# A hybrid mixer step on one Trainium2 core: beta multiplied into the decays on GpSimd, wider VectorE products, shorter scale computation

## The chip, the cores and the metric

The kernel runs on one core of one Trainium2 chip. Its engines are TensorE (PE, matrix products; PEld is its weight load), VectorE (DVE), ScalarE (ACT), GpSimd (POOL) and SyncE (SP, which here issues DMA transfers). Each engine runs its own instructions in order; waits between engines are by semaphores. SBUF is the working memory, PSUM takes TensorE's results. The metric is the device time of one execution in microseconds.

## The reference

One layer of a hybrid backbone for 128 context tokens and 2048 sample tokens, model width 1024. The input is normed and modulated, then one projection feeds three branches; each is gated by SiLU of another projection, projected back, weighted by a sigmoid gate, and the sum goes through an output projection and a residual.

```python
qkv, beta, dec, z_a, u_b, v_b, z_b, x_c, z_c, gates = jnp.split(proj, points, axis=-1)
# A: chunked gated DeltaNet, forward and backward
m = eye + bc[..., :, None] * jnp.einsum('bnhik,bnhjk->bnhij', kc, kc) * dec_strict
sol = lax.linalg.triangular_solve(m, rhs, left_side=True, lower=True, unit_diagonal=True)
qk = jnp.einsum('bnhik,bnhjk->bnhij', qc, kc) * dec_incl
# B: spatial gating in chunks of 128 tokens
vn = rmsnorm(v, g_norm).reshape(B, n, CHUNK_B, G_B, CH_B)
vs = jnp.einsum('gpq,bnqgc->bnpgc', w_s, vn) + b_s.T[None, None, :, :, None]
o_b = u * vs.reshape(B, T, W_BR) * jax.nn.silu(z_b)
# C: Fourier mixing of x_c, times silu(z_c)
pb = jnp.einsum('btnw,nwd->btnd', br, w_branch)
merged = jnp.einsum('btnd,btnd->btd', jax.nn.sigmoid(gates), pb)
out = jnp.einsum('btd,de->bte', merged, w_out)
```

## The kernel before

All products of float32 data are made of float16 pairs (a high and a low half, three products per block). To make the halves of a weight tile, `converting` (L198) squares it on ScalarE (L209, with the sum per partition in `ss`), turns the sum into bfloat16 on VectorE (`widened`, L173), sums it over the partitions with a product by ones, and `scales` (L178) takes from the exponent bits of the result a power of two `s` and its inverse: a copy out of PSUM (L183), a shift (L185), and a multiply-add of integers for each (L186, L187). `w.inv` is the inverse times `isx`, the inverse scale of the normed input (L216). Then ScalarE writes the high half (L218) and VectorE the low one (L219). This is done for 93 weight tiles; `scales` alone also serves the input, the branches, the bounds of the delta branch and the 17 blocks before the output projection.

The stages, in order of time: modulation, the normed input and z_A (to about 120 us), the q/k/v projection with its short convolution and the decays (to about 440 us), V, U and z_B of branch B, x_C and z_C with the Fourier products, the gates and branch products (`merge`), and the output projection.

The delta branch runs beside these as a generator whose steps `Pace` releases in proportion to the products written, `delta` (L1079). For each of 17 chunks of 128 tokens, `prep` (L681) loads q, k, v and the decays `dc` (`decay_rows`, L761, one chunk ahead), norms k (`norm` L693, with the inverse square root on GpSimd, L698, and `tok`, L707), transposes it (L723), makes K K^T in PSUM, and for each of two directions multiplies it by beta and the decay, head by head (L738, four instructions), copies the diagonal blocks (L740), and splits the result into halves (L742, L743). The blocks `nd` leave through two DMA issues on GpSimd's queue (L748). Then the products of q and k take the decays (L754) and are split (L756, L757). `n_` and `q_` share three buffers of tag `n32`. Between chunks, `base_inverse` (L766) inverts the diagonal blocks of a group by many small VectorE operations (L787, L788). Then `scan` goes over the chunks in both directions with its chain of products.

In branch B, `spatial` (L1155) multiplies the normed values of a chunk by the spatial weights, and adds the bias per group (L1161, four instructions, in which the norm's weight `sgug(g)` multiplies the product, channel by channel on the partitions). The values themselves are scaled by the inverse root mean square before (L1188).

A scheduler orders the instructions of each engine from the program, by dependences and buffers; `tc.high_priority()` and `tc.issue_after()` guide it. So a change in one place can move instructions elsewhere.

Of the kernel before, what the change touches and what calls it, by code (L numbers as in the profile page):

```python
# [12 lines left out]
I32 = mybir.dt.int32  # L13
# [7 lines left out]
P = 128  # L21
# [90 lines left out]
def hybrid_flow_kernel(ctx: ExitStack, tc: tile.TileContext, x_prompt, x_sample, state_delta, c, c_ctx, ln_g, w_ada,  # L112
# [62 lines left out]
        V.tensor_copy(sb16, ss)  # L175
        return sb16

    def scales(ss, pl, tag, sb16=None):  # L178

        ps = bank(ps_x, [P, 1])  # L180
        mm(ps, ones16, widened(ss, pl, tag) if sb16 is None else sb16)
        t = sb(pl, [P, 4], tag)
        V.tensor_copy(t[:, 0:1], ps)  # L183
        h = t[:, 3:4].bitcast(I32)
        V.tensor_scalar(h, t[:, 0:1].bitcast(I32), 24, None, ALU.logical_shift_right)  # L185
        V.tensor_scalar(t[:, 1:2].bitcast(I32), h, -8388608.0, 204.0 * 8388608, ALU.mult, ALU.add)  # L186
        V.tensor_scalar(t[:, 2:3].bitcast(I32), h, 8388608.0, 50.0 * 8388608, ALU.mult, ALU.add)  # L187
        return t[:, 1:2], t[:, 2:3]

    def load_w(src, nkt, cols=P, hi=None, lo=None, tag="w", bufs=5):  # L190
        return convert(read_w(src, nkt, cols, tag), nkt, cols, hi, lo, tag, bufs)
# [6 lines left out]
    def converting(w, st, nkt, cols=P, hi=None, lo=None, tag="w", bufs=5):  # L198

        wpool = bwp[0] if tag == "b" else wp  # L200
        if tag == "z":
            hi, lo = [sb(p0p, [P, nkt, cols], n_, F16, bufs=4) for n_ in ("zhi", "zlo")]
        if tag == "v":
            hi, lo = [t[:, vfilled[0]] for t in v4]
            vfilled[0] += 1
        w.hi = sb(wpool, [P, nkt, cols], tag + "hi", F16, bufs=bufs) if hi is None else hi
        w.lo = sb(wpool, [P, nkt, cols], tag + "lo", F16, bufs=bufs) if lo is None else lo
        ss = sb(wp, [P, 1], "wss", bufs=4)
        A.activation(w.lo, st, AF.Square, accum_out=ss)  # L209
        yield  # L210
        sb16 = widened(ss, wp, "wsc")
        if wnext[0] < 11:
            yield
        s, inv = scales(None, wp, "wsc", sb16)
        w.inv = sb(wp, [P, 1], "winv", bufs=10)
        V.tensor_mul(w.inv, inv, isx)  # L216
        yield
        A.activation(w.hi, st, AF.Copy, scale=s)  # L218
        V.scalar_tensor_tensor(w.lo, st, s, w.hi, ALU.mult, ALU.subtract)  # L219
# [143 lines left out]
        V.tensor_copy(pc, pp)  # L363

    convw = lambda j, ct: pc[:, 8 + j * 12 + ct:8 + j * 12 + ct + 1]
    sgug = lambda g: pc[:, 44 + g:45 + g]
    ong = pc[:, 48:49]


# [44 lines left out]
    with tc.high_priority():  # L414
# [7 lines left out]
        A.activation(bnd[:, 1, :], sh.rearrange("p k g -> p (k g)"), AF.Square, scale=math.sqrt(2.0), accum_out=bss[:, 1:2])  # L422
        V.tensor_add(bss[:, 2:3], bss[:, 0:1], bss[:, 1:2])
        sx, isx = scales(bss[:, 2:3], cp, "xsc")
        V.tensor_scalar(ms, ms, sx, None, ALU.mult)
        V.tensor_scalar(sh, sh, sx, None, ALU.mult)

# [46 lines left out]
    def h3(ap):  # L474
        return ap.rearrange("p (h x) -> p h x", h=H)
# [205 lines left out]
    def prep(g, ci, t, nxt, held):  # L681
# [49 lines left out]
        pair = lambda t_, h: (t_[:, 0, hs(h)], t_[:, 1, hs(h)])  # L731
        for h in range(H):
            mm3(ps[:, hs(h)], pair(T, h), pair(T, h))
        nd = sb(d2, [P, 2, H, 32], "nd", bufs=2)
        for d in range(2):
            n_ = sb(d2, [P, WB], "n32", bufs=3)
            for h in range(H):
                V.scalar_tensor_tensor(n_[:, hs(h)], ps[:, hs(h)], beta[:, d, t, h:h + 1], dc[:, d, hs(h)], ALU.mult, ALU.mult)  # L738
            for B in range(4):
                A.copy(nd[32 * B:32 * B + 32, d], h3(n_)[32 * B:32 * B + 32, :, 32 * B:32 * B + 32])  # L740
            n16 = sb(d2, [P, 2, WB], "n16", F16, bufs=4)
            made = A.activation(n16[:, 0, :], n_, AF.Copy, scale=FS)  # L742
            V.scalar_tensor_tensor(n16[:, 1, :], n_, FS, n16[:, 0, :], ALU.mult, ALU.subtract)  # L743
            late([(nD[d][t], n16)], made)
            yield 1
# [6 lines left out]
        for d in range(2):  # L752
# [3 lines left out]
            made = A.activation(p16[:, 0, :], q_, AF.Copy, scale=1.0 / FS)  # L756
            V.scalar_tensor_tensor(p16[:, 1, :], q_, 1.0 / FS, p16[:, 0, :], ALU.mult, ALU.subtract)  # L757
            late([(qkD[d][t], p16)], made)
            yield 1

    def decay_rows(t):  # L761
        dc = sb(dq, [P, 2, WB], "dc", bufs=2)
        SY.dma_start(dc, decD[t])
        return dc

    def base_inverse(g):  # L766
        nt = len(GROUPS[g])
# [311 lines left out]
    def delta():  # L1079
        nonlocal dq  # L1080
        seq = [(g, ci, t) for g, ts in enumerate(GROUPS) for ci, t in enumerate(ts)]
        held = {1: rows(1, 16), 2: rows(2, 16), 0: rows(0, 16), "dc": decay_rows(16)}
        yield from bounds()
        base = iter(())
        for i_, (g, ci, t) in enumerate(seq):
# [58 lines left out]
    bsp = sb(bp, [P, 4, P], "bsp", bufs=1)  # L1144
    SY.dma_start(bsp, b_spatial[0].rearrange("g (o p) -> o g p", o=1).to_broadcast([P, 4, P]))
    wsT = sb(bp, [P, 4, P], "wsT", bufs=1)
    vw = getw(4, 3)
    ps = bank(ps_x, [P, 4, P])
    for g in range(4):
# [3 lines left out]
    for i in range(4):  # L1153
        V.tensor_copy(vinv[:, i:i + 1], vw[i].inv)
    def spatial(t, vn):  # L1155
        vs = sb(bp, [P, 4, P], "vs", bufs=4)
        ps = bank(ps_x, [P, 4, P])
        for g in range(4):
            mm(ps[:, g, :], vn[:, g, :], wsT[:, g, :])
        for g in range(4):  # L1160
            V.scalar_tensor_tensor(vs[:, g, :], ps[:, g, :], sgug(g), bsp[:, g, :], ALU.mult, ALU.add)  # L1161
        vout.append((t, vs))

    def vstore(made):
# [5 lines left out]
    for t in range(NCH):  # L1170
# [12 lines left out]
        rsqrt(ss, ss, 1.0 / WB, 1)  # L1183
        if vprev is not None:
            spatial(*vprev)
        if len(vout) > 2:
            vstore(made)
        V.tensor_scalar(vn, vn, ss, None, ALU.mult)  # L1188
        vprev = (t, vn)
        if t == 8:  # L1190
            SY.dma_start(cf, consts[:, _CF:_CW])
# [366 lines left out]
```

## Time and profile before

| what | value |
|---|---|
| runs: median (lowest to highest of 3) | 2199.03 us (2198.21 to 2199.14) |
| profiled execution: span from the first to the last instruction | 2198.9 us |
| mean granted clock of TensorE | 0.994 |
| moved by DMA | 365.04 MB, mean 166 GB/s |
| instructions L738 / L1161 / L1188 on VectorE | 136 / 68 / 17 |
| weight tiles converted | 93 |

The page of a profile gives each engine's busy time and its share of the span; further views give groups of instructions (line, engine, operation, output and inputs, shapes, count, busy us, mean ns of one, idle time of the engine before them and what ended it), who waited for whom, the busy time by stretch of time, and instructions in order of time. Durations of instructions that follow each other can overlap by a part, so several in a row take less than their sum. The lines that matter are in the prediction.

### The profile page before, as it was taken

The numbers are of one execution on the slowest core, as the hardware profiler recorded it, in microseconds if no ns is written. First come the engines' busy times: TensorE is split into PE (matmuls) and PEld (weight loads), VectorE is DVE, ScalarE is ACT, GpSimd is POOL, SyncE is SP. The second block draws the span as 40 slices with busy tenths as digits, with TensorE's granted clock in tenths as the row PEclk, the third lists the DMA queues.
The fourth block names the chain that finished last, engine by engine and source line by source line (L and its number), as shares of the span: only waits on it lengthen the run. The fifth ranks groups of instructions, "written<-read, shape, count | busy, mean of one in ns | idle before, by whom it ended". The sixth has DMA issues, their size and how long they took to land.

```text
span 2198.9 us, 41979 instructions
## 1 busy us (share of the span) xinstructions
PE 2133.4 (97%) x15990; PEld 1231.3 (56%) x15990; DVE 1297.7 (59%) x3085; ACT 1007.5 (46%) x2325; POOL 713.8 (32%) x861
## 2 busy tenths in 40 slices
PE   7999999999999999999899999999999999999998
PEld 3565444455555587878555556555655444444444
DVE  5746745479878796455665555756574444233454
ACT  3644644355555563344644445755553422222332
POOL 1421433223334322432312233255442222122553
PEclk9999999999999999999999999999999999999999
DMA  8434733167777654433655556766664544433542
GB/s 279 142 99 156 252 117 111 60 206 220 238 224 237 205 166 110 123 115 115 219 171 165 161 168 187 235 186 212 213 207 147 172 125 123 124 101 110 180 153 105
DMA packets 304275, 365.04 MB, mean 166 GB/s; under 512 B 39393, under 2 KB 215754, under 8 KB 302026
## 3 DMA queue, kind: packets, MB, share of 16 engines
q1 hardware_dynamic: 251690, 267.38, 40.5%
q0 software_dynamic: 12688, 51.27, 6.5%
q10 hardware_dynamic: 39696, 43.72, 5.8%
q8 instruction: 125, 2.05, 0.4%
q14 instruction: 76, 0.62, 0.1%
HBM read 234.67 MB, written 127.62 MB: 165 GB/s over the span
## 4 chain that ended last, share of the span: by engine, by line
PE 47%; DMA 6%; DVE 5%; ACT 3%; issue 1%; POOL 1%; SPq 0%; ACTq 0%; POOLq 0%; DVEq 0%
PE b L161 47%; DMA st<-br 2%; DMA wst<-in_w_branch_dram 1%; DMA wst<-in_w_in_dram 1%; DMA mt<-mrg 1%; DVE E L788 1%; DVE XB L787 1%; DMA ei<-XB 0%; DMA skn<-kv 0%; DMA br<-o 0%; ACT big L1336 0%; DMA XB<-nd 0%; ACT XB L793 0%; DVE big L1337 0%; DVE u L904 0%
## 5 line engine op out<-in xcount | busy, mean ns | idle before, releaser
L161 PE MATMUL b<-xh,whi 128*128 128x512 f16 (+1 forms) x1920 | 650.5, 347 | 7.7 <-DVE sg L1125 5.0
L161 PE MATMUL b<-xl,whi 128*128 128x512 f16 (+1 forms) x1920 | 650.8, 347 | 0.0
L161 PE MATMUL b<-xh,wlo 128*128 128x512 f16 (+1 forms) x1920 | 650.2, 347 | 0.4 <-DVE wlo L219 0.4
L161 PEld LDWEIGHTS <-whi 128*128 128x128 f16 x3904 | 356.4, 98 | 335.2 <-issue 13.7
L161 PEld LDWEIGHTS <-wlo 128*128 128x128 f16 x1952 | 191.1, 98 | 178.8 <-issue 1.3
L161 PE MATMUL b<-big,bhi 128*128 128x512 f16 (+1 forms) x960 | 250.5, 347 | 1.5 <-DVE big L1337 1.1
L1376 POOL TENSOR_TENSOR mrow<-mrow,sg 128x512 f32<-128x512 f32 (+1 forms) x80 | 95.0, 1187 | 288.4 <-DVE sg L1375 163.6
L161 PE MATMUL b<-big,blo 128*128 128x512 f16 (+1 forms) x480 | 163.3, 347 | 0.0
L1366 ACT ACTIVATE sg<-b,winv 128x512 f32<-128x512 f32 (+1 forms) x120 | 74.2, 619 | 153.9 <-PE b L161 153.4
L628 POOL TENSOR_TENSOR cy<-cy,raw 128x545 f32<-128x545 f32 (+1 forms) x48 | 74.5, 1580 | 184.4 <-ACT raw L627 184.4
L161 PEld LDWEIGHTS <-xh 128*128 128x128 f16 x1496 | 117.1, 98 | 29.9 <-issue 1.5
L161 PEld LDWEIGHTS <-bhi 128*128 128x128 f16 x960 | 87.0, 98 | 76.0 <-ACT big L1336 0.3
L175 DVE CAST wscb<-wss 128x1 bf16<-128x1 f32 x93 | 14.3, 154 | 190.9 <-ACT wlo L209 83.4
L1375 DVE SCALAR_TENSOR_TENSOR sg<-b,binv,sg 128x512 f32<-128x512 f32 (+1 forms) x80 | 53.4, 668 | 102.3 <-PE b L161 90.9
L860 POOL COPY T<-ES 32x256 f16<-32x256 f16 x68 | 28.5, 419 | 208.2 <-DMA ES<-ei 179.3
L161 PE MATMUL b<-whi,xl 128*128 128x128 f16 x544 | 93.0, 219 | 0.0
L161 PE MATMUL b<-whi,xh 128*128 128x128 f16 x544 | 93.0, 219 | 0.0
L161 PE MATMUL b<-wlo,xh 128*128 128x128 f16 x544 | 93.0, 219 | 0.0
L161 PE MATMUL b<-wohi,mh 128*128 128x512 f16 (+2 forms) x248 | 91.9, 372 | 0.6 <-ACT mh L1446 0.6
L161 PE MATMUL b<-wohi,ml 128*128 128x512 f16 (+2 forms) x248 | 91.7, 372 | 0.3 <-DVE ml L1447 0.3
L161 PE MATMUL b<-wolo,mh 128*128 128x512 f16 (+2 forms) x248 | 91.9, 372 | 0.0
L219 DVE SCALAR_TENSOR_TENSOR wlo<-wst,wsc,whi 128x1024 f16<-128x1024 f32 x52 | 72.4, 1396 | 31.6 <-ACT whi L218 31.3
(455 smaller groups left out, 4281.2 us busy)
## 6 DMA issues: line engine op xcount, KB each, us to landing
wst<-in_w_in_dram SPq DMA_DIRECT2D x60, 512.0 KB, 5.5
qkv<-cy POOLq DMA_DIRECT2D x12, 1089.0 KB, 5.2
st<-br SPq DMA_DIRECT2D x48, 256.0 KB, 4.6
mrow<-mrg SPq DMA_DIRECT2D x18, 512.0 KB, 4.0
mrow<-mrg SPq DMA_DIRECT2D x16, 576.0 KB, 4.5
mrg<-mrow POOLq DMA_DIRECT2D x16, 576.0 KB, 3.7
dc<-dec SPq DMA_DIRECT2D x17, 512.0 KB
kq<-qkv SPq DMA_DIRECT2D x34, 256.0 KB, 4.8
```

What stands on the lines that cost most here:

```text
L161: PE.matmul(out, l, r, start=start, stop=stop)
L175: V.tensor_copy(sb16, ss)
L219: V.scalar_tensor_tensor(w.lo, st, s, w.hi, ALU.mult, ALU.subtract)
L628: G.tensor_tensor(y[:, c0:c1], y[:, c0:c1], raw[:, 1 + c0:1 + c1], ALU.mult)
L787: V.tensor_tensor(t3, X3[:, 0:k, k:k + 1].to_broadcast([P, k, n_]), E3[:, k:k + 1, k:32].to_broadcast([P, k, n_]), ALU.mult)
L788: V.tensor_tensor(E3[:, 0:k, k:32], E3[:, 0:k, k:32], t3, ALU.subtract)
L860: G.tensor_copy(T16[rows(a0, b), :, :, b], ES[0:32, :, 2 * a0 + b, :, wT])
L1366: A.activation(sg, ps, AF.Sigmoid, scale=gw.inv)
L1375: V.scalar_tensor_tensor(sg, ps, binv[:, 1:2], sg, ALU.mult, ALU.mult)
L1376: G.tensor_tensor(mr, mr, sg, ALU.add)
```

## The change

Three parts.

1. `weighted` is new: two GpSimd products per chunk multiply the decays of both directions by beta (broadcast over 128 columns) into two `n32` tiles. It is called at the end of the chunk before, for the next one; `prep` then multiplies K K^T in PSUM by that tile in one instruction of 512 columns per direction, in place.
2. The norm's weight of branch B is loaded as a tile broadcast over the partitions (`sgb`) and multiplied into the values together with their scale; the spatial result then needs one addition of the bias over all four groups. `vs` has three buffers, and its store is issued when two are waiting.
3. The squares of a weight are summed straight into bfloat16, the exponent is shifted straight out of PSUM, and the inverse scale of the input is folded in as exponent bits (`xbits`), so that `w.inv` comes from the multiply-add itself.

```diff
-    def scales(ss, pl, tag, sb16=None):
+    def scales(ss, pl, tag, sb16=None, inv=None):
...
-        V.tensor_copy(t[:, 0:1], ps)
         h = t[:, 3:4].bitcast(I32)
-        V.tensor_scalar(h, t[:, 0:1].bitcast(I32), 24, None, ALU.logical_shift_right)
+        V.tensor_scalar(h, ps.bitcast(I32), 24, None, ALU.logical_shift_right)
         V.tensor_scalar(t[:, 1:2].bitcast(I32), h, -8388608.0, 204.0 * 8388608, ALU.mult, ALU.add)
-        V.tensor_scalar(t[:, 2:3].bitcast(I32), h, 8388608.0, 50.0 * 8388608, ALU.mult, ALU.add)
-        return t[:, 1:2], t[:, 2:3]
+        if inv is None:
+            inv = t[:, 2:3]
+            V.tensor_scalar(inv.bitcast(I32), h, 8388608.0, 50.0 * 8388608, ALU.mult, ALU.add)
+        else:
+            V.tensor_scalar(inv.bitcast(I32), h, 8388608.0, xbits, ALU.mult, ALU.add)
+        return t[:, 1:2], inv
...
-        ss = sb(wp, [P, 1], "wss", bufs=4)
-        A.activation(w.lo, st, AF.Square, accum_out=ss)
+        ss = sb(wp, [P, 1], "wss", BF16, bufs=4)
+        with nc.allow_low_precision(reason="the sum only sets a power of two"):
+            A.activation(w.lo, st, AF.Square, accum_out=ss)
         yield
-        sb16 = widened(ss, wp, "wsc")
         if wnext[0] < 11:
             yield
-        s, inv = scales(None, wp, "wsc", sb16)
         w.inv = sb(wp, [P, 1], "winv", bufs=10)
-        V.tensor_mul(w.inv, inv, isx)
+        s, _ = scales(None, wp, "wsc", ss, w.inv)
...
         sx, isx = scales(bss[:, 2:3], cp, "xsc")
+        xbits = sb(cp, [P, 1], "xbits")
+        V.tensor_scalar(xbits, isx.bitcast(I32), -77.0 * 8388608, None, ALU.add)
...
+        db = cur["db"]
         nd = sb(d2, [P, 2, H, 32], "nd", bufs=2)
         for d in range(2):
-            n_ = sb(d2, [P, WB], "n32", bufs=3)
-            for h in range(H):
-                V.scalar_tensor_tensor(n_[:, hs(h)], ps[:, hs(h)], beta[:, d, t, h:h + 1], dc[:, d, hs(h)], ALU.mult, ALU.mult)
+            n_ = db[d]
+            V.tensor_mul(n_, ps, n_)
...
             late([(qkD[d][t], p16)], made)
+            if d:
+                more("db", lambda: weighted(nxt, held["dc"]))
             yield 1
...
+    def weighted(t, dc):
+        db = [sb(d2, [P, WB], "n32", bufs=3) for _ in range(2)]
+        for d in range(2):
+            G.tensor_tensor(h3(db[d]), h3(dc[:, d, :]), bc(beta[:, d, t, :], P), ALU.mult)
+        return db
...
         held = {1: rows(1, 16), 2: rows(2, 16), 0: rows(0, 16), "dc": decay_rows(16)}
+        held["db"] = weighted(16, held["dc"])
...
+    sgb = sb(bp, [P, 4, P], "sgb", bufs=1)
+    SY.dma_start(sgb, sgu_norm_g.rearrange("o (g p) -> o g p", g=4).to_broadcast([P, 4, P]))
...
-        vs = sb(bp, [P, 4, P], "vs", bufs=4)
+        vs = sb(bp, [P, 4, P], "vs", bufs=3)
...
-        for g in range(4):
-            V.scalar_tensor_tensor(vs[:, g, :], ps[:, g, :], sgug(g), bsp[:, g, :], ALU.mult, ALU.add)
+        V.tensor_tensor(vs, ps, bsp, ALU.add)
...
-        if len(vout) > 2:
+        if len(vout) > 1:
             vstore(made)
-        V.tensor_scalar(vn, vn, ss, None, ALU.mult)
+        V.scalar_tensor_tensor(vn, vn, ss, sgb, ALU.mult, ALU.mult)
```

More of the change, by code (lines that the diff above doesn't have):

```diff
@@ L365, in hybrid_flow_kernel @@
     convw = lambda j, ct: pc[:, 8 + j * 12 + ct:8 + j * 12 + ct + 1]
-    sgug = lambda g: pc[:, 44 + g:45 + g]
     ong = pc[:, 48:49]
```

## The prediction

> **What bounds the kernel now.** I read the first page, then the busy time of each engine by stretch, then what TensorE waited for.
>
> ```profile
> span 2198.9 us, 41979 instructions
> PE 2133.4 (97%) x15990; PEld 1231.3 (56%) x15990; DVE 1297.7 (59%) x3085; ACT 1007.5 (46%) x2325; POOL 713.8 (32%) x861
> ...
> 0.00:80.00 80.00, 62.85 (x304) 30.07 (x305) 47.95 (x119) 35.75 (x66) 21.26 (x25) 0.94 0.76 243
> 80.00:440.00 360.00, 359.63 (x2246) 183.85 (x2245) 201.84 (x274) 174.45 (x264) 113.40 (x127) 1.00 0.39 132
> 440.00:900.00 460.00, 439.97 (x3403) 284.09 (x3402) 367.60 (x964) 247.66 (x729) 139.81 (x181) 0.99 0.64 194
> 900.00:1700.00 800.00, 779.97 (x7444) 498.99 (x7444) 470.24 (x1220) 403.09 (x1035) 288.03 (x394) 1.00 0.58 178
> 1700.00:2100.00 400.00, 399.04 (x2144) 191.36 (x2143) 162.97 (x416) 118.87 (x187) 108.12 (x100) 1.00 0.44 136
> 2100.00:2199.00 99.00, 91.98 (x457) 42.96 (x454) 47.09 (x93) 27.64 (x44) 43.15 (x37) 0.98 0.37 125
> ...
> 500.00:600.00 100.00, 95.06 (x593) 55.23 (x592) 90.07 (x242) 48.15 (x152) 32.46 (x42) 1.00 0.73 233
> ```
>
> The columns of the stretches are the time, then the busy time of PE, PEld, DVE, ACT and POOL, the granted clock, the DMA share and GB/s. TensorE is the bound: busy 2133.4 of 2198.9 us at a clock of 0.94 to 1.00. The change adds and removes no matmul, so it can win only from the 65.5 us in which TensorE is idle. These lie in four places: 17.2 us at the start (80 - 62.85), 20.0 us in 440:900 (chunk preparation, beside the V, U and Fourier products), 20.0 us in 900:1700 (the scan, beside the merges), 7.0 us behind the last product. In 440:900 VectorE is the fullest helper: 367.6 of 460 us, and 90 of 100 us in 500:600. That is where this change takes most from it. What TensorE waited for, in us, times, longest (the last row is VectorE's, in 440:860):
>
> ```profile
> PE b L161 <- ACT S L903: 5.3, 3, 2.3
> PE b L161 <- DVE sg L1125: 5.0, 2, 3.0
> PE b L723 <- DVE tok L707: 4.3, 2, 2.5
> PE b L161 <- DVE Q L891: 4.0, 2, 2.9
> PE b L161 <- DVE vrow L1213: 2.7, 1, 2.7
> PE b L455 <- DVE wsc L186: 2.6, 2, 1.6
> PE b L161 <- DVE T L725: 1.7, 1, 1.7
> PE b L161 <- DVE wlo L219: 0.4, 1, 0.4
> ...
> DVE sg L1125 <- ACT sg L1123: 13.1, 6, 4.0
> ```
>
> Of the 20.0 us in 440:900, sg L1125, tok L707, vrow L1213 and T L725 are 13.7 us: all on VectorE. S L903 and Q L891 belong to the scan; wsc L186 to the start.
>
> **Masked products (L738).** Per chunk and direction four products of 128x128 become one of 128x512; the tile `n_` already holds decay times beta.
>
> ```profile
> 647.01 2.16 DVE L738 SCALAR_TENSOR_TENSOR n<-b,beta,dc 128x128 f32<-128x128 f32 x8 [2.00 <-PE b L161]
> 650.68 1.28 DVE L754 TENSOR_TENSOR n<-b,dc 128x512 f32<-128x512 f32 x2
> L738 DVE SCALAR_TENSOR_TENSOR n<-b,beta,dc 128x128 f32<-128x128 f32 x136 | 36.9, 341 | 2.1 <-PE b L161 2.0
> ```
>
> One of the old takes 341 ns, but eight in a row take 2.16 us, as starts overlap ends. The new form stands in the trace already, as L754: PSUM times an SBUF tile of that width, two in 1.28 us. So 0.88 us per chunk, times 17 (136/8) = 15.0 us off VectorE.
>
> **Spatial values (L1161, L1188).**
>
> ```profile
> 469.85 1.11 DVE L1161 SCALAR_TENSOR_TENSOR vs<-b,pc,bsp 128x128 f32<-128x128 f32 x4
> L1188 DVE TENSOR_SCALAR sg<-sg,vss 128x512 f32<-128x512 f32 x17 | 8.5, 497 | 2.6 <-POOL vss L171 2.5
> L716 DVE SCALAR_TENSOR_TENSOR q<-qr,qsc,q 128x512 f16<-128x512 f32 x17 | 12.6, 743 | 3.1 <-ACT q L715 3.1
> ```
>
> Four additions in 1.11 us become one, which I price at half of L754's pair, 0.64 us: 0.47 x 17 = 8.0 us off. The norm weight moves into L1188, which gets a second SBUF tensor; L716 is that form, 743 ns against 497: 0.25 x 17 = 4.2 us on. Net 3.8 us off. The broadcast load of the norm weight is one more 256 KB transfer on SP before the first product of this stage: nothing, as SP's loads run ahead there (the decays' below, by a chunk). `vs` has three buffers for four, but a store now leaves when two wait instead of three; I take nothing.
>
> **Scales.** Per weight the cast L175, the PSUM copy L183 and the product L216 go; the exponent is shifted straight out of PSUM, which I price as L183's own PSUM read.
>
> ```profile
> L175 DVE CAST wscb<-wss 128x1 bf16<-128x1 f32 x93 | 14.3, 154 | 190.9 <-ACT wlo L209 83.4 <-ACT wolo L209 43.7 <-ACT blo L209 43.0
> L183 DVE COPY wsc<-b 128x1 f32<-128x1 f32 x93 | 13.6, 149 | 23.3 <-PE b L161 23.2
> L216 DVE TENSOR_TENSOR winv<-wsc,xsc 128x1 f32<-128x1 f32 x93 | 33.9, 366 | 2.0
> L219 DVE SCALAR_TENSOR_TENSOR wlo<-wst,wsc,whi 128x1024 f16<-128x1024 f32 x12 | 15.3, 1277 | 4.1 <-ACT whi L218 4.1
> 49.95 1.12 DVE L216 TENSOR_TENSOR winv<-wsc,xsc 128x1 f32<-128x1 f32 x1
> ```
>
> 154 + 149 + 366 = 0.67 us per weight, 62 us of VectorE over 93 weights. The last but one row counts the weights converted in 440:860: 12, so 8.0 us there. Weights are converted well ahead of use (TensorE waits 0.4 us in all for their low halves), so outside 440:900 this buys little. At the start it does: the first scale stands before the first modulated tile. One copy of about 0.15 us leaves that chain, though `xbits` joins VectorE's queue ahead of that tile (0.15 us), and a product that took 1.12 us (L216 at 49.95) leaves from in front of the second weight's low half. Between 0 and 1.3 us; I take 0.5, nearer the copy than the product, since TensorE's wait on the scales is 2.6 us in all and belongs to the first tile. In the closing stage the copy goes 17 times, hidden by products of 400 us with 1.0 us idle.
>
> **GpSimd's new work.** 34 products of 128x512 with beta broadcast. The trace has the very form:
>
> ```profile
> L966 POOL TENSOR_TENSOR skn<-skn,ed 128x512 f32<-128x512 f32 x34 | 37.3, 1096 | 121.0 <-DMA skn<-kv 118.2 <-DVE o L920 2.8
> 472.19 0.76 POOL L748 DMA_DIRECT2D nd<-nd  x1 [1.42 <-ACT nd L740]
> 472.97 1.21 POOL L698 TENSOR_TENSOR ss<-ss,mhalf 128x4 f32<-128x4 f32 x1
> 473.90 0.33 SPq L763 DMA_DIRECT2D dc<-dec  x1
> 473.91 0.68 DVE L757 SCALAR_TENSOR_TENSOR n<-n,n 128x512 f16<-128x512 f32 x1
> 475.18 0.68 DVE L707 TENSOR_TENSOR tok<-b,ss 128x512 f32<-128x512 f32 x1
> 682.86 1.08 POOL L698 TENSOR_TENSOR ss<-ss,mhalf 128x4 f32<-128x4 f32 x1 [0.38 <-DVE ss L697]
> ```
>
> 34 x 1.10 = 37.3 us on GpSimd, which is busy 139.8 of 460 us there: room. In the built order the pair stands behind the two `nd` DMA issues and ahead of the next chunk's inverse square root L698, so what is behind it is L698, then `tok` L707 on VectorE, then TensorE's transposes of it. Its decays are not late: their load leaves SP at 473.90, when the chunk before has read the buffer, a whole chunk ahead. Its second tile is: `n32` has three buffers, and it gets the one that L757 frees at 474.6. So in this chunk the pair would run 472.95 to 474.05 and 474.6 to 475.7, and L698 would end at 476.9 where it ended at 474.2. `tok` had 1.0 us to spare (475.18), so it comes 1.7 us late. Five of the chunks have L698 this close behind `nd` (first and last above); elsewhere GpSimd idles there. In the built order TensorE has its transposes of `tok` on average 13 large products later than before, so it does other products meanwhile; I take nothing for it, and 5 x 1.7 = 8.5 us if that cover fails.
>
> The other price is the SBUF path:
>
> ```profile
> L697 DVE TENSOR_SCALAR ss<-ss x34: 151/161/1844, 456.3 to 826.4; 128x4 f32<-128x4 f32 x34
> 679.11 0.33 DVE L787 TENSOR_TENSOR XB<-XB,E 128x175 f32<-128x175 f32 x1
> 680.02 1.35 DVE L788 TENSOR_TENSOR E<-E,XB 128x175 f32<-128x175 f32 x1
> 679.38 1.80 POOL L1135 TENSOR_TENSOR st<-sg,vrow 128x512 f32<-128x512 f32 x1
> ```
>
> At 680 us a VectorE operation of two SBUF tiles took 1.35 us where its like took 0.33, beneath a GpSimd product that was itself stretched; L697 ranges from a median of 161 ns to 1844. So a new GpSimd product costs VectorE between 0 and 1.0 us, 0 to 34 us in all. I take 0.35, a third, since only operations of some kinds are caught and GpSimd sometimes waits instead: 12 us.
> The Trainium skill, "GPSIMD Engine Reference", section "Specifications", says that GpSimd's SBUF interface is shared with VectorE and contended by VectorE's two-port modes and by its instructions with two SBUF inputs. By that rule L216 leaves the contest, the new L1188 joins it, and the masked product (one input in PSUM) stays out; were each new product to block VectorE for its whole 1.10 us, 37 us would come on, and the relief would be gone, which is the first rival below. The two operations at 680 us agree with it.
>
> **The sum.** VectorE in 440:900: -15.0 - 3.8 - 8.0 + 12 = -14.8 us, 4% of its 367.6. VectorE's sg itself waits for ScalarE's sigmoid (13.1 us), so of TensorE's 13.7 us of waits on VectorE I let not all go, but the 8.7 that are not sg's in their larger part: 5.5 us, between 0 and 13.7. Start: 0.5. Scan: VectorE is busy 59% there and the operations in the recurrence are the same, so 1 us of its 20. Together 7.0: 2198.9 - 7.0 = 2191.9. The span is 0.1 us below the median of the runs, so 2192.
>
> **The rivals.**
> 1. *GpSimd in the way (slower).* The pair delays L698, and with it `tok`, by 1.7 us in five chunks, 8.5 us, and its SBUF traffic eats VectorE's relief. It decides from 27/34 = 0.79 us of blocking per product (15.0 + 3.8 + 8.0 = 26.8). With the start's gain: 2199 + 8.5 - 0.5 = 2207. For: VectorE at 90% in 500:600, and the stretched pair at 680 us. Against: GpSimd idles behind `nd` in most chunks, and TensorE's later place for the transposes.
> 2. *Hidden anyway.* The waits for sg follow ScalarE's queue, those for tok move with the new order, and the sum of idle stays within 4 us: 2196 to 2202, say 2199. For: a mean of 4% of VectorE's time is little. Against: four separate waits on VectorE in this stretch.
> 3. *The scan's order (slower).* The instructions of all engines are placed anew; in the built order the products of the recurrence stand on average 5 large products earlier on TensorE. A product of the stretch 80:440 takes 0.16 us (359.63 / 2246), so 0.8 us earlier. Where a step has nothing to spare, TensorE then waits that long: in half of the 34 steps, 13.6 us, less the 6.0 of the rest: 2199 + 7.6 = 2206. Against: what leaves VectorE's queue, 0.67 us per weight, leaves it in this stage too, and most steps show no wait (S L903 three, Q L891 two).
> 4. *More of it.* All 13.7 us of waits on VectorE go, and 4 of the scan's for it (Q L891): 2199 - 18 = 2181.
>
> **Chances.** Forecast 0.42 (its own range 2186 to 2195); rival 4 0.10; rival 2 0.20; rival 1 0.18; rival 3 0.10. A measurement of this kernel can tell about 0.2%, 4.4 us, from no change. So faster 0.52, same 0.20, slower 0.28. Range: from 2184, most of the way to rival 4, to 2208, just past rivals 1 and 3, which together hold too much to be left out.
>
> **What would show it.** Right: in 440:900 TensorE's idle falls from 20.0 to about 14 us with VectorE's busy time near 350; eight L738 become two of 0.64 us; GpSimd's products near 1.1 us, no wait of theirs on the decays; L697 and L788 with a mean hardly above today's. Wrong: a new wait of TensorE on `tok` L707 or of VectorE on L698; GpSimd's products at 1.5 us and more; or idle in 900:1700 that grows beyond 25 us.

## The result, and the profile after

The changed kernel took 2209.66 us (median of 5 runs, 2205.68 to 2211.99) beside 2199.14 us before (5 runs, 2198.21 to 2201.49): ratio 1.0039, 95% interval 1.0022 to 1.0055. It is slower by some 0.4%, where 2192 us, a gain of 0.3%, had been forecast.

The first page of the profile after, and the busy time by stretch:

```profile
span 2206.6 us, 41612 instructions
PE 2137.4 (97%) x15990; PEld 1230.5 (56%) x15990; DVE 1267.0 (57%) x2631; ACT 1006.4 (46%) x2325; POOL 750.3 (34%) x895
```

```profile
0.00:80.00 80.00, 65.66 (x307) 31.29 (x308) 49.13 (x105) 36.90 (x68) 24.56 (x27) 0.94 0.76 245
80.00:440.00 360.00, 360.00 (x2248) 183.94 (x2247) 192.30 (x222) 175.47 (x263) 103.69 (x125) 1.00 0.39 131
440.00:900.00 460.00, 434.67 (x3347) 276.68 (x3346) 359.56 (x758) 239.45 (x720) 180.76 (x213) 0.99 0.64 193
900.00:1700.00 800.00, 777.71 (x7454) 500.34 (x7453) 463.24 (x1124) 404.89 (x1040) 288.02 (x392) 1.00 0.59 177
1700.00:2100.00 400.00, 399.51 (x2148) 191.74 (x2147) 150.07 (x330) 119.80 (x188) 107.73 (x100) 1.00 0.43 135
```

VectorE ran 454 instructions fewer and 31 us less in all. Yet TensorE's idle time in 440:900 is 25.3 us (460 - 434.67) where it was 20.0. GpSimd has 41 us more there. Fixed stretches hide where the time is lost, since the work in them shifts. Better marks are products that both kernels contain: the last that reads `v4hi` (the V weights) and the first that reads `Y` (the Fourier stage). Between these lie the U and z_B products, beside which most chunks are prepared. First before, then after (duration min/median/max, first and last start):

```profile
L161 PE MATMUL b<-v4hi,xh x136: 377/379/379, 428.1 to 546.1; 128*128 128x512 f16 x136
L161 PE MATMUL b<-cf,Y x128: 272/275/377, 806.4 to 1043.2; 128*128 128x128 f32 x128
```

```profile
L161 PE MATMUL b<-v4hi,xh x136: 376/379/379, 426.8 to 545.1; 128*128 128x512 f16 x136
L161 PE MATMUL b<-cf,Y x128: 272/275/377, 818.1 to 1052.7; 128*128 128x128 f32 x128
```

Up to 546 us the changed kernel is 1.0 us ahead. Then 546.1 to 806.4 (260.3 us) becomes 545.1 to 818.1 (273.0 us): 12.7 us lost. From the first Y to the end of the span it is 1392.5 us before and 1388.5 after: 4.0 us gained. -1.0 + 12.7 - 4.0 = +7.7, the whole difference of the spans. I call 546 to 818 us "the stage" from here on. Its windows, before and after:

```profile
546.10:806.40 260.30, 249.02 (x1907) 153.18 (x1906) 210.19 (x523) 148.63 (x442) 92.31 (x116) 0.99 0.71 219
```

```profile
545.10:818.10 273.00, 252.36 (x1907) 153.35 (x1906) 213.20 (x420) 146.99 (x448) 119.19 (x140) 0.99 0.69 210
```

The same 1907 products; TensorE's idle time goes from 11.3 to 20.6 us, and its busy time is 3.3 us longer. For these same products it lies between 247 and 257 us in the runs below, and goes with the granted clock: 247.3 and 248.2 us where the row shows 1.00 (e8, e6), 256.5 us where it shows 0.97 (e15). Why the clock differs was not followed. VectorE has 103 instructions fewer and is nevertheless 3 us busier. What TensorE waited for in the stage after:

```profile
PE b L726 <- DVE tok L710: 7.0, 4, 3.1
PE b L161 <- DVE sg L1137: 4.5, 2, 3.1
PE b L693 <- issue: 3.0, 2, 1.8
PE b L161 <- DVE T L728: 2.3, 2, 1.2
PE b L161 <- DVE sg L1201: 1.9, 1, 1.9
```

And for `tok` before, in its stage:

```profile
PE b L723 <- DVE tok L707: 1.8, 1, 1.8
```

The wait for `tok` (L710, L707 before) has grown from 1.8 us in this stage, once, to 7.0 us, four times (in all of 440:900 from 4.3 to 7.0 us). The longest, at 718 us, can be followed back. VectorE's instructions in order of time, then GpSimd's (start, us; the wait before it in brackets):

```profile
709.23 0.69 DVE L760 SCALAR_TENSOR_TENSOR n<-n,n 128x512 f16<-128x512 f32 x1
709.83 2.67 DVE L798 TENSOR_TENSOR XB<-XB,E 128x231 f32<-128x231 f32 x1
712.42 0.74 DVE L1137 SCALAR_TENSOR_TENSOR sg<-b,winv,sg 128x512 f32<-128x512 f32 x1
713.08 0.16 DVE L700 TENSOR_SCALAR ss<-ss 128x4 f32<-128x4 f32 x1
...
713.46 1.75 DVE L760 SCALAR_TENSOR_TENSOR n<-n,n 128x512 f16<-128x512 f32 x1
715.14 0.74 DVE L719 SCALAR_TENSOR_TENSOR q<-qr,qsc,q 128x512 f16<-128x512 f32 x1
715.80 0.37 DVE L798 TENSOR_TENSOR XB<-XB,E 128x220 f32<-128x220 f32 x1
...
717.59 0.68 DVE L710 TENSOR_TENSOR tok<-b,ss 128x512 f32<-128x512 f32 x1
```

```profile
710.19 2.04 POOL L774 TENSOR_TENSOR n<-dc,beta 128x512 f32<-128x512 f32 x2
713.24 1.42 POOL L1147 TENSOR_TENSOR st<-sg,vrow 128x512 f32<-128x512 f32 x1 [1.01 <-DVE ss L700]
```

A small inversion step of VectorE, L798, takes 2.67 us where its like six microseconds later takes 0.37: it ends when the pair of new GpSimd products (L774, 710.19 to 712.23) has ended. Behind it in VectorE's queue stand sg L1137, L700 and `tok`, all late by the 2.3 us. A further L760 is then stretched from 0.69 to 1.75 us beneath a GpSimd product that was there before (L1147). TensorE reaches the transposes of `tok` first and waits 3.1 us.

### The profile page after: what moved, and what is told of

The parts are those of the page before. It is cut to its first block, busy times and chain, and to the rows that moved or that the text cites. A ratio compares the mean times of both kernels' runs of the same rounds, so it can differ in the third digit from the quotient of the medians.

```text
span 2206.6 us, 41612 instructions
## 1 busy us (share of the span) xinstructions
PE 2137.4 (97%) x15990; PEld 1230.5 (56%) x15990; DVE 1267.0 (57%) x2631; ACT 1006.4 (46%) x2325; POOL 750.3 (34%) x895
## 5 line engine op out<-in xcount | busy, mean ns | idle before, releaser
L631 POOL TENSOR_TENSOR cy<-cy,raw 128x545 f32<-128x545 f32 (+1 forms) x48 | 66.9, 1422 | 185.2 <-ACT raw L630 185.2
L221 DVE SCALAR_TENSOR_TENSOR wlo<-wst,wsc,whi 128x1024 f16<-128x1024 f32 x52 | 73.6, 1417 | 38.7 <-ACT whi L220 38.3
L161 PE MATMUL b<-wohi,ml 128*128 128x512 f16 (+2 forms) x248 | 91.7, 372 | 0.5 <-DVE ml L1460 0.5
L213 ACT ACTIVATE wlo<-wst 128x1024 f16<-128x1024 f32 x52 | 54.9, 1056 | 68.9 <-DMA wst<-in_w_in_dram 57.8
```

The source lines that it names most:

```text
L161: PE.matmul(out, l, r, start=start, stop=stop)
L631: G.tensor_tensor(y[:, c0:c1], y[:, c0:c1], raw[:, 1 + c0:1 + c1], ALU.mult)
```

## The experiments

Fifteen kernels. "Idle" is TensorE's idle time in the stage; each stage has its own marks. Ratios are to the kernel before on the same chip; the other numbers are from the one profiled execution. From chip to chip the kernel before takes 2199 to 2203 us at the median; the times in the expectations of e1 to e4 start from 2199, and on their chip it takes 2202.0 us.

| run | ratio, 95% interval | stage, us | idle | VectorE busy | GpSimd busy |
|---|---|---|---|---|---|
| before | 1 | 260.3 | 11.3 | 210.2 | 92.3 |
| after | 1.0039, 1.0022 to 1.0055 | 273.0 | 20.6 | 213.2 | 119.2 |
| e1 part 1 alone | 1.0052, 1.0037 to 1.0068 | 273.2 | 18.0 | 213.9 | 119.5 |
| e2 parts 2 and 3 | 0.9974, 0.9964 to 0.9985 | 263.2 | 11.7 | 209.9 | 90.9 |
| e3 weights on VectorE | 1.0021, 1.0008 to 1.0035 | 264.6 | 13.3 | 211.8 | 93.7 |
| e4 weights on ScalarE | 1.0010, 0.9997 to 1.0024 | 269.4 | 17.1 | 201.6 | 91.6 |
| e5 e2 + spare products | 1.0057, 1.0035 to 1.0079 | 273.0 | 20.7 | 220.0 | 120.2 |
| e6 e2 + spare powers | 0.9993, 0.9980 to 1.0007 | 258.6 | 10.5 | 208.6 | 91.0 |
| e7 products early | 1.0035, 1.0024 to 1.0047 | 271.3 | 19.2 | 213.5 | 119.0 |
| e8 part 3 alone | 0.9955, 0.9940 to 0.9970 | 258.5 | 11.2 | 208.5 | 90.8 |
| e9 wide operation alone | 0.9984, 0.9974 to 0.9993 | 264.0 | 12.7 | 201.1 | 90.8 |
| e10 part 2 alone | 1.0002, 0.9991 to 1.0013 | 264.3 | 13.6 | 212.9 | 92.8 |
| e11 weights stored | 1.0074, 1.0061 to 1.0087 | 265.4 | 13.0 | 199.8 | 91.7 |
| e12 part 3 again | 0.9969, 0.9956 to 0.9981 | 262.5 | 12.0 | 208.6 | 90.6 |
| e13 powers pinned | 0.9997, 0.9987 to 1.0008 | 261.3 | 11.4 | 208.9 | 117.3 |
| e14 spare products behind | 1.0040, 1.0028 to 1.0053 | 270.8 | 17.4 | 219.0 | 121.0 |
| e15 weights behind | 1.0052, 1.0039 to 1.0064 | 275.8 | 19.3 | 209.2 | 122.2 |

Wherever large GpSimd products run in the stage, idle is 17 to 21 us; elsewhere it is 10 to 14, but for e4. So a difference of 2 or 3 us between two of these rows says nothing by itself.

**Which part costs (e1, e2).** e1 is the kernel before with part 1; e2 is the changed kernel with part 1 undone.

> The kernel before with part 1 alone (beta times decays on GpSimd, one wide masked product). Theory A, GpSimd's products block VectorE over the SBUF path and hold back the inverse square root behind them, so tok comes late for TensorE: this part alone carries the loss, 2206 to 2212 us, with TensorE waiting 6 us or more on tok (4.3 before) and single VectorE operations of two SBUF tiles at 2 us and more. Theory B, the new order of all instructions is what costs, whichever part brings it: this part alone lands anywhere from 2194 to 2206, and its place has nothing to do with GpSimd's products.

> The changed kernel with part 1 undone: masked products head by head on VectorE as before, parts 2 and 3 kept. Theory A: the loss goes, 2192 to 2199 us, and TensorE's idle in 440:900 is at most the 20.0 us of before. Theory B: also this order differs from the one before, so 2200 to 2210 is as likely as not.

Part 1 alone loses 0.5%, parts 2 and 3 gain 0.3%. The loss is part 1's. e1 lies where theory A had it (1.0052 of 2199 us is 2210), with VectorE operations of two SBUF tiles at 2.24 and 2.84 us, but not by way of `tok`: TensorE waits for it 4.7 us in all, for 4.3 before, where 6 or more were expected.

**The weighting on another engine (e3, e4).** In `weighted`, in place of GpSimd's product, e3 and then e4:

```diff
-            G.tensor_tensor(h3(db[d]), h3(dc[:, d, :]), bc(beta[:, d, t, :], P), ALU.mult)
+            V.tensor_tensor(h3(db[d]), h3(dc[:, d, :]), bc(beta[:, d, t, :], P), ALU.mult)
```

```diff
-            G.tensor_tensor(h3(db[d]), h3(dc[:, d, :]), bc(beta[:, d, t, :], P), ALU.mult)
+            for h in range(H):
+                A.activation(db[d][:, hs(h)], dc[:, d, hs(h)], AF.Copy, scale=beta[:, d, t, h:h + 1])
```

> The changed kernel with the two products of decay and beta on VectorE, everything else kept. VectorE pays two products of two SBUF tiles per chunk, 1.28 us by L754's pair, against 0.88 saved: 0.4 us x 17 = 7 us more of VectorE than before in this stage, less 8.0 and 3.8 of the other parts. Theory A: GpSimd is out of the way, so 2195 to 2202 us although VectorE is fuller than in the changed kernel. If instead VectorE's fullness decided, it would be slower than the changed kernel: above 2210.

> The changed kernel with the products of decay and beta on ScalarE, eight activations of 128 columns per chunk with beta as scale (about 0.29 us each, 2.3 us per chunk). VectorE keeps its relief and GpSimd has nothing of it. Theory A: 2190 to 2199 us, the best of the four. Theory B: no better than the others. If ScalarE's queue in front of the sigmoids decides (VectorE waited 13.1 us for them before): above 2203, with longer waits for L1123's sigmoid.

Both beat the changed kernel's stage: 264.6 and 269.4 us for 273.0. Neither beats e2. In e3 the stage is nearly as without the weighting, though VectorE has to do it itself, and 1.0021 stems from behind it: from the first Y to the end it takes 1397.0 us, with a wait of TensorE for ScalarE's `xc` of 4.5 us (2.4 before); why that grew I did not follow. In e4 ScalarE has 172.8 us of work in the stage for 147 (0.40 us for each of the new operations, where 0.29 was expected), and idle is 17.1 us. By their ratios (2204 and 2201 us where the kernel before takes 2199) both missed the times of theory A by some 2 us. ScalarE's queue, the third case for e4, does not show either: VectorE's waits for the sigmoid are no longer in sum (12.5 us in the stage for 13.1). So moving the work off GpSimd helps the stage, and the place for it on ScalarE is no better than that on VectorE.

**Traffic or queue (e5, e6, e7).** Two ways remain in which GpSimd's products can delay VectorE: they stop its operations (theory A1), or they stand ahead of the inverse square root L701 in GpSimd's queue, for which `tok` waits (A2). e5 and e6 put spare work into e2, with a result that nobody reads; VectorE's masked products stay as before. e7 calls `weighted` earlier, and for the chunk itself. At the end of `prep` e5 adds:

```diff
+            if d and nxt is not None:
+                for e, a, n in ((0, 0, 3), (1, 0, 3), (1, 2, 2)):
+                    x = sb(d2, [P, 3, P], "spare", F16, bufs=1)
+                    G.tensor_tensor(x[:, 0:n, :], h3(held["dc"][:, e, :])[:, a:a + n, :], beta[:, e, nxt, a:a + n].rearrange("p (h o) -> p h o", o=1).to_broadcast([P, n, P]), ALU.mult)
```

e6 in the same place:

```diff
+            if d and nxt is not None:
+                for e in range(2):
+                    x = sb(d2, [P, H], "spare", bufs=1)
+                    G.tensor_tensor(x, egl[:, e, nxt, :], mhalf.to_broadcast([P, H]), ALU.pow)
```

And e7, beside the loss of the call at the end:

```diff
         G.tensor_scalar(rq[:, t, :], ss[:, 0, :], P ** -0.5, None, ALU.mult)
+        db = weighted(t, cur["dc"])
```

> Parts 2 and 3 of the change alone (the version that took 0.9974 of the time before), and at the end of each chunk's preparation three spare GpSimd products of 128x384, 128x384 and 128x256 columns (half-precision result that nobody reads, some 2 us in all), in the very place of the two new products; VectorE's masked products stay eight. Theory A1 (their SBUF traffic stops VectorE): about what part 1 cost, ratio 1.002 to 1.004, last v4hi to first Y near 273 us, VectorE operations of two SBUF inputs stretched above 2 us beneath them. Theory A2 (they stand ahead of the inverse square root L701 in GpSimd's queue): the same time here, but then the run with short spare operations (e6) must cost as much. Rival B (the wide masked product and the buffers held from the chunk before cost the time, not GpSimd's work): ratio stays near 0.9975 and the stage near 263 us.

> Parts 2 and 3 alone, and in the place of the two new products two spare GpSimd power operations of 128x4 (each about 1.1 us by L701's mean, almost no SBUF traffic; the result is not read). Theory A1 (SBUF traffic): ratio 0.997 to 0.998, last v4hi to first Y near 263 us as without them. Theory A2 (place in GpSimd's queue): ratio 1.001 to 1.004, that stage 268 to 273 us, L701 late and TensorE waiting for tok. Rival B: as A1.

> The whole change, but the two GpSimd products of a chunk are issued in that chunk's own preparation, just behind the scaling of q's inverse norm, so that they stand behind L701 of that chunk in GpSimd's queue and ahead of its kv store; nothing is made a chunk ahead. Theory A1 (SBUF traffic): the loss mostly stays, ratio 1.001 to 1.004, stage 268 to 273 us, VectorE still stretched beneath the products. Theory A2 (queue): ratio 0.995 to 0.998, stage 260 to 263 us, no wait of TensorE on tok above the 4.3 us before. Rival B: ratio 0.995 to 0.998 as well if it is the buffers held a chunk ahead, else as A1.

e5 reproduces the whole loss with nothing but spare products (1.0057), so neither the wide operation nor the buffers held from the chunk before (rival B) are needed for it. e6 and e7 do not tell A1 from A2: e6's ratio (0.9993) lies between the two ranges, and in both the GpSimd work ran elsewhere than intended. The rows of the spare powers in e6:

```profile
L765 POOL TENSOR_TENSOR spare<-egl,mhalf x32: 997/1009/1955, 443.2 to 495.5; 128x4 f32<-128x4 f32 x32
```

All 32 ran in 443 to 496 us: they depend on nothing late, and the scheduler placed them ahead of the chunks. In e7 it did the reverse: the products have all they need when the chunk before ends, and stood again ahead of L701:

```profile
707.44 2.04 POOL L772 TENSOR_TENSOR n<-dc,beta 128x512 f32<-128x512 f32 x2
710.49 1.42 POOL L1144 TENSOR_TENSOR st<-sg,vrow 128x512 f32<-128x512 f32 x1 [1.01 <-DVE ss L700]
711.88 1.49 POOL L701 TENSOR_TENSOR ss<-ss,mhalf 128x4 f32<-128x4 f32 x1
```

**What the parts are worth (e8 to e12).** e8 and e12 are part 3 alone, e10 part 2 alone. e9 is e2 with the masked product as one wide operation that needs no weights. It leaves out the factor beta, so its results are not the layer's:

```diff
-            for h in range(H):
-                V.scalar_tensor_tensor(n_[:, hs(h)], ps[:, hs(h)], beta[:, d, t, h:h + 1], dc[:, d, hs(h)], ALU.mult, ALU.mult)
+            V.scalar_tensor_tensor(n_, ps, 0.5 / (FS * FS), dc[:, d, :], ALU.mult, ALU.mult)
```

e11 has parts 1 and 3, but makes the weighted decays in the decay stage and loads them:

```diff
+        def flush2(t, row):
+            for d in range(2):
+                G.tensor_tensor(row[:, d], row[:, d], beta[:, d, t, :].rearrange("p (h o) -> p h o", o=1).to_broadcast([P, H, P]), ALU.mult)
+            G.dma_start(decB[t], row.rearrange("p d h i -> p d (h i)"))
...
-            G.tensor_tensor(h3(db[d]), h3(dc[:, d, :]), bc(beta[:, d, t, :], P), ALU.mult)
+            SY.dma_start(db[d], decB[t][:, d, :])
```

> Part 3 alone (three operations fewer per weight's scale). If the gain of the version without the products (ratio 0.9974) is the scales', the ratio is 0.997 to 0.998 and the start's milestones come 0.5 to 1 us earlier; if it is the spatial values', it stays within 0.9995 to 1.0005.

> Parts 2 and 3, and the masked product of K K^T in one wide VectorE operation per direction, but with a constant half in place of beta, so that nothing has to weight the decays (the factor beta is left out of this product). It shows what the wide operation is worth without GpSimd's work. Theory A1 (GpSimd's SBUF traffic is the whole loss): at or below the version without part 1, ratio 0.993 to 0.9975, last v4hi to first Y 255 to 263 us, VectorE some 10 us less busy there. Rival B (the wide operation itself sits badly, for TensorE or for ScalarE behind it): ratio 1.000 or more, stage above 266 us.

> Part 2 alone. The scales alone took 0.9955 [0.994, 0.997], scales and spatial values together 0.9974 [0.9964, 0.9985]. If the two add up, part 2 alone is a small loss: ratio 1.000 to 1.003. If the difference between those is chance, it is a gain of up to 4 us as forecast: 0.998 to 1.000.

> Parts 1 and 3, but the weighted decays are made while the decays are made (80 to 440 us, GpSimd, in place behind the store of the plain ones, then a second store), and each chunk loads them into the two buffers that part 1 filled by GpSimd. Theory A1: VectorE is no longer stopped in 440 to 818 us, so below the scales alone if the wide operation is worth something and the 17.8 MB more of transfers do not collide: ratio 0.991 to 0.996. Rival (transfers: the DMA share is 0.7 in 545 to 806 us already): loads of weights, decays or q, k, v come late, ratio 1.000 or more.

> Part 3 alone once more, on the chip of the other three, to compare with: ratio 0.994 to 0.997 as before; stage last v4hi to first Y 258 to 261 us.

Part 3 gains 0.3% (e12) to 0.45% (e8, more than expected). Together with part 2 it gained 0.26%, but the intervals touch, and part 2 alone neither gains nor loses (1.0002): that it costs anything is not shown. e12's stage, 262.5 us, was longer than the 258 to 261 expected. The stage of e2, then of e9:

```profile
544.50:807.70 263.20, 251.54 (x1907) 154.35 (x1906) 209.94 (x492) 149.14 (x445) 90.90 (x116) 0.99 0.70 218
```

```profile
544.90:808.90 264.00, 251.30 (x1908) 153.45 (x1906) 201.09 (x421) 146.71 (x445) 90.75 (x116) 0.99 0.70 216
```

The wide operation takes 8.9 us off VectorE, and TensorE's idle time does not fall (11.7 to 12.7 us). VectorE's relief came as expected; ratio (0.9984) and stage missed the expectation, and the relief shows no worth here. e11 agrees: VectorE at 199.8 us, idle 13.0. Its own loss lies in 80:440, where GpSimd now makes the weights:

```profile
80.00:440.00 360.00, 344.66 (x2133) 174.63 (x2132) 209.87 (x213) 168.94 (x254) 159.81 (x171) 0.98 0.44 153
```

TensorE, idle for 0.4 us there before, is idle for 15.3 us, and the first V product starts at 446.1 for 428.1 us. The transfers in the stage, which were the rival, did no harm (idle 13.0 at a DMA share of 0.75). The loss in 80:440 has the same look: there GpSimd's 34 products run beside VectorE's own products of the decays (L606, two SBUF tiles), which take 2.27 us (`dc`) and 2.66 us (`XB`) on the mean, where their like in e12 (L598) take 1.34 and 1.22. VectorE is busy 209.9 us for 191.0. No run varied this.

**Traffic or queue, pinned (e13, e14, e15).** The spare powers now read the next chunk's decays, so that they can't start before those have landed; the spare products read q's inverse norm, so that both L701 of the chunk are past; and the change's own products are tied behind it.

e13, e14 and e15 in this order (`made` is the line of `rq` before it):

```diff
-                    G.tensor_tensor(x, egl[:, e, nxt, :], mhalf.to_broadcast([P, H]), ALU.pow)
+                    G.tensor_tensor(x, egl[:, e, nxt, :], held["dc"][:, e, 0:H], ALU.pow)
```

```diff
         G.tensor_scalar(rq[:, t, :], ss[:, 0, :], P ** -0.5, None, ALU.mult)
+        for e, a, n in ((0, 0, 3), (1, 0, 3), (1, 2, 2)):
+            x = sb(d2, [P, 3, P], "spare", F16, bufs=1)
+            G.tensor_tensor(x[:, 0:n, :], h3(cur["dc"][:, e, :])[:, a:a + n, :], rq[:, t, a:a + n].rearrange("p (h o) -> p h o", o=1).to_broadcast([P, n, P]), ALU.mult)
```

```diff
+        with tc.issue_after(made.ins):
+            db = weighted(t, cur["dc"])
```

> Parts 2 and 3 alone, and per chunk two spare GpSimd powers of 128x4 that read the next chunk's decays, so that they can't run before these have landed and stand where e5's spare products stood (some 2.1 us per chunk, almost no SBUF traffic). A1 (SBUF traffic): ratio 0.996 to 0.999, TensorE idle 10 to 13 us between last v4hi and first Y, VectorE's means unchanged (L760 near 0.69 us). A2 (place in GpSimd's queue): ratio 1.002 to 1.006, idle 17 to 21 us, waits for tok above 6 us.

> Parts 2 and 3 alone, and e5's three spare products per chunk (128x384, 128x384, 128x256, half-precision result, not read), which multiply the chunk's decays by q's inverse norm, so that they stand behind both L701 of their chunk in GpSimd's queue. A1: TensorE idle 16 to 21 us between last v4hi and first Y and ratio 1.001 to 1.006, as in e5; VectorE some 10 us busier than without them. A2: idle 10 to 13 us, ratio 0.996 to 0.999.

> The whole change with its two products per chunk tied behind q's inverse norm of their own chunk, so that L701 never waits for them; in exchange the masked product may have to wait for them. A1: ratio 1.001 to 1.006, idle 16 to 21 us. A2: ratio 0.995 to 0.999, idle 10 to 13 us, and no wait for tok above the 3 to 4 us without products.

The rows of e13's powers, and its stage:

```profile
L765 POOL TENSOR_TENSOR spare<-egl,dc x32: 997/1032/1937, 443.0 to 792.5; 128x4 f32<-128x4 f32 x32
```

```profile
545.00:806.30 261.30, 249.91 (x1907) 154.02 (x1906) 208.89 (x490) 148.35 (x441) 117.30 (x141) 0.99 0.70 219
```

Now the powers stand in place (443 to 793 us), and GpSimd is as busy in the stage as with the products: 117.3 us. TensorE's idle is 11.4 us, VectorE's time that of e2. `tok` waits longer for L701 there (7.1 us in VectorE's queue, for 1.9 in e2), and TensorE still waits only 2.2 us for `tok`. The ratio, 0.9997, lies above A1's range and some 0.2% above e2's (0.9974, on another chip), so occupying GpSimd may cost something too; the profiled execution (2197.1 us) is one of the fastest of the 11, whose median is 2202.9, so its rows can't show where. Beneath two of the powers, VectorE's operations of two SBUF tiles keep their usual time:

```profile
685.19 2.16 POOL L765 TENSOR_TENSOR spare<-egl,dc 128x4 f32<-128x4 f32 x2 [2.69 <-DMA dc<-dec]
685.52 0.67 DVE L760 SCALAR_TENSOR_TENSOR n<-n,n 128x512 f16<-128x512 f32 x1
686.12 0.36 DVE L794 TENSOR_TENSOR XB<-XB,E 128x207 f32<-128x207 f32 x1
686.51 0.38 DVE L795 TENSOR_TENSOR E<-E,XB 128x207 f32<-128x207 f32 x1
```

e14's stage:

```profile
547.30:818.10 270.80, 253.45 (x1908) 154.79 (x1907) 219.04 (x485) 148.41 (x441) 121.01 (x153) 0.98 0.68 211
```

The same spare products as in e5, now behind L701, cost the same: VectorE 9.1 us busier than in e2, idle 17.4 us, ratio 1.0040. And e15 keeps the loss although L701 stands ahead of its chunk's products and the masked product never waits for them. In e14 and e15 TensorE waits for `tok` 2.4 and 3.1 us in the stage, no longer than in e2 (3.1); the loss shows in its waits for sg, T and other results of VectorE. A1 holds, A2 falls: the products stop VectorE wherever they stand. That the data they move does it, and not another difference between these products and the powers, is argued; no run varied one without the other.

Which of VectorE's operations are stopped in the changed kernel shows in their means. VectorE's groups of e13 in 440:820 (busy us, mean ns), and below those of the changed kernel:

```profile
L760 DVE SCALAR_TENSOR_TENSOR n<-n,n 128x512 f16<-128x512 f32 x32 | 22.1, 692 | 6.4 <-ACT n L759 6.4
L757 DVE TENSOR_TENSOR n<-b,dc 128x512 f32<-128x512 f32 x32 | 21.5, 682 | 0.0
L221 DVE SCALAR_TENSOR_TENSOR wlo<-wst,wsc,whi 128x1024 f16<-128x1024 f32 x12 | 15.4, 1280 | 5.1 <-ACT whi L220 5.1
L719 DVE SCALAR_TENSOR_TENSOR q<-qr,qsc,q 128x512 f16<-128x512 f32 x17 | 12.7, 744 | 0.6 <-ACT q L718 0.6
L728 DVE SCALAR_TENSOR_TENSOR T<-b,T 128x512 f16<-128x512 f32 x16 | 11.0, 686 | 2.1 <-ACT T L727 2.0
```

```profile
L760 DVE SCALAR_TENSOR_TENSOR n<-n,n 128x512 f16<-128x512 f32 x30 | 25.7, 857 | 7.3 <-ACT n L759 7.3
L741 DVE TENSOR_TENSOR n<-b,n 128x512 f32<-128x512 f32 x32 | 20.5, 682 | 3.7 <-PE b L161 3.7
L757 DVE TENSOR_TENSOR n<-b,dc 128x512 f32<-128x512 f32 x30 | 20.2, 682 | 0.1
L221 DVE SCALAR_TENSOR_TENSOR wlo<-wst,wsc,whi 128x1024 f16<-128x1024 f32 x12 | 17.6, 1470 | 5.1 <-ACT whi L220 4.8
L719 DVE SCALAR_TENSOR_TENSOR q<-qr,qsc,q 128x512 f16<-128x512 f32 x16 | 14.3, 896 | 0.5 <-ACT q L718 0.5
...
L728 DVE SCALAR_TENSOR_TENSOR T<-b,T 128x512 f16<-128x512 f32 x16 | 10.9, 683 | 1.6 <-ACT T L727 1.6
```

L760, L221 and L719 read two tiles in SBUF: 692 to 857, 1280 to 1470, 744 to 896 ns on the mean. (L221 alone would prove little: in e4, without the products, its mean is 1546.) L757 and L728, with one operand in PSUM (`b`), stay at 682 and 683 to 686.
The Trainium skill, "GPSIMD Engine Reference", section "Specifications", names instructions with two SBUF inputs as those that contend with GpSimd; the trace agrees for these five.

Where the products stand elsewhere, others are hit. In e14 L760's and L719's like keep their means (697 and 743 ns in the stage), and the excess lies on the small inversion steps, which read two SBUF tiles as well. Their rows of e2 in its stage, then of e14:

```profile
L791 DVE TENSOR_TENSOR E<-E,XB 128x220 f32<-128x220 f32 (+15 forms) x88 | 33.1, 376 | 1.4
L790 DVE TENSOR_TENSOR XB<-XB,E 128x207 f32<-128x207 f32 (+15 forms) x87 | 31.8, 365 | 2.1
```

```profile
L794 DVE TENSOR_TENSOR E<-E,XB 128x220 f32<-128x220 f32 (+15 forms) x88 | 38.3, 435 | 1.4
L793 DVE TENSOR_TENSOR XB<-XB,E 128x207 f32<-128x207 f32 (+15 forms) x87 | 36.9, 424 | 2.1
```

These two rows grow by 10.3 us, the whole of what VectorE has more in e14's stage.

## Why the prediction was wrong

**The bound** held: TensorE's idle time beside chunk preparation decided the result, and the operations' prices were near. Two masked products take 1.28 us, as priced; L1174 takes 0.68 us (priced 0.64) and L1201 0.75 (priced 0.74).

**The step that failed is the sum in VectorE's time.** I added reliefs and stalls of VectorE to one figure, -14.8 us, and turned that into -5.5 us of TensorE's idle. In 440:900 idle rose by 5.3 us instead. Relief and stall do not exchange at one rate. e9 took 8.9 us of relief and gave no idle time back. The products put 12.1 us on VectorE in the stage (213.2 after, 201.1 in e9, with 420 and 421 instructions) and 7.9 us on TensorE's idle (20.6 against 12.7): two thirds of each stalled microsecond. The other versions with large products, each against e2 or e9, give between half (e7) and nine tenths (e5). The rows at 709.83 show how: the stall falls in one piece of 2.3 us in front of a row of queued operations, and `tok` is among them, for which TensorE waits next. The relief came in pieces of 0.88 us per chunk, and TensorE's waits did not get shorter by them in sum (e9).

**The price of the stall** itself was under-sized, but by less than would matter. 24 more GpSimd operations stand in the stage (140 less 116), so 12.1 / 24 = 0.50 us for each, 17 us over 34, where 0.35 and 12 us were taken. In the forecast's own sum 5 us more would still have left a relief of 9.8 us. In e15 the same products cost 8.1 us over 25 operations, 0.32 us each, and the idle time was as long.

**The first rival, "GpSimd in the way"**, gave 2207 us; measured were 2209.66. One of its two halves held, the traffic. Its other half, the pair ahead of L698, is not what costs (e13, e15), and so neither is "5 x 1.7 us" the way to its number, whose nearness is chance. `tok` does come late in the changed kernel, by 5.2 us more of TensorE's waits in the stage. The longest of them goes back to VectorE's own queue; VectorE's `tok` waits for L701 3.4 us there, for 1.9 before. Its point of decision, 0.79 us of stall per product, was wrong for the reason above: it was the point at which VectorE's sums are equal. At 0.50 us the kernel was already slower, and so was e15 at 0.32. A chance of 0.18 was too low for a rival with two stretched operations in the quoted rows.

**Parts 2 and 3.** The spatial values' -3.8 us of VectorE were again worth nothing (e10). The load of the norm weight, for which nothing was taken, held VectorE for 2.7 us, until 448.8 us, ahead of the stage that loses. The scales were undersized: 0.5 us at the start and their share of the -5.5; measured were 6.8 us (e12, 0.31% of 2203) and 9.9 us (e8). In e12's profile, 4.4 us shorter than the one before, 1.1 us lie ahead of the last V product and 5.5 us behind the first Y (1387.0 us to the end for 1392.5), while the stage between is 2.2 us longer. I had written that outside 440:900 they buy little; which wait they shorten there was not traced.

**The other rivals.** *Hidden anyway* describes the reliefs of parts 1 and 2. *The scan's order* does not show: from the first Y on the changed kernel is 4.0 us faster. *More of it* does not show either.

**The signs I had named.** Idle near 14 us in 440:900: it was 25.3, which decides against the forecast, as does the named new wait on `tok`. VectorE near 350 us there: 359.6. GpSimd's products near 1.1 us: their median is 1.096, their mean in 440:820 1.21, the longest 1.72. Idle in 900:1700: 22.3 us, below the 25 named. No wait of theirs on the decays: right; they wait for the buffers.

The fastest version is part 3 alone: 0.9969 and 0.9955 of the time before.

## What to carry to other kernels

An operation given to GpSimd beside a busy VectorE has to be priced by what it stops there: here 0.3 to 0.5 us of VectorE per product of 1.1 us, on operations with two tiles in SBUF, and between half and nine tenths of that ended up as idle time of TensorE. Relief and stalls of a helper engine are not one sum: a stall counts at the queue position where it falls, and relief counts only where the bound engine waits for that very operation. A probe must be tied by its data to the place that it is to test; here the scheduler moved two of them away or back.

## What had not been expected

Two kinds of GpSimd operation of about the same duration differ widely in what they cost VectorE: 32 powers of 128x4, 1.09 us each, left VectorE's busy time in the stage as it was (e13: 208.9 us, e2: 209.9), and products of 128x384 and 128x256, 0.88 and 0.67 us each, put 9 us on it (e14). The duration of a GpSimd operation is no measure of what it stops.

In e13 the powers read SBUF too.
The Trainium skill, "SBUF — State Buffer", section "SBUF: two separate sides", has the shared port held for a GpSimd instruction's whole duration. L798's 2.67 us beneath two products agrees with the length of the hold, though the page gives the port to whichever starts first, and L798's record starts 0.36 us ahead of the products'. The powers do not agree: beneath two of them, 2.16 us long, L760 took 0.67 us and XB 0.36.
